# A hybrid RWKV-7 / RG-LRU layer with a Strassen MLP on one core: splits of the features spread over a pair's steps with four rooms, weights loaded by halves, and another issue order at the change of stages and in the last group

## The chip, the cores and the metric

One Trainium2 chip, one of its eight cores. The time is device time in microseconds of one launch, the median of several runs. TensorE (PE) multiplies matrices into PSUM, VectorE (DVE) and ScalarE (ACT) work on tiles, GpSimd (POOL) does elementwise work on tiles outside PSUM, SyncE (SP) issues nearly all transfers. Each of them takes its instructions in program order.

## What is computed

One trunk layer over 128 context tokens and 1024 latent tokens, all float32. The change touches its last part, the MLP, whose hidden width is 4096 over a model width of 1024:

```python
x = x + gate1 * rms_norm(y, lp['g_post_mix'])
h = rms_norm(x, lp['g_pre_mlp']) * (1.0 + scale2) + shift2
f = jnp.square(jax.nn.relu(jnp.einsum('btd,df->btf', h, lp['w_mlp1'])))
f = jnp.einsum('btf,fd->btd', f, lp['w_mlp2'])
x = x + gate2 * rms_norm(f, lp['g_post_mlp'])
```

Before it stand an input projection, a bidirectional delta-rule recurrence on 8 heads, a bidirectional gated linear recurrence on 512 channels and an output projection; they take the first 950 us and are not touched, but for one number (the size of GpSimd's descriptor ring).

## The kernel before

Every operand of a matmul is split in two parts of reduced precision, a high one (`H`, a copy by ACT) and the rest (`L`, a subtraction by DVE, or by GpSimd in the second product); a product is three matmuls (HH, HL, LH). To save matmuls, both MLP products use a Strassen-Winograd scheme with seven products instead of eight, so sums of blocks are formed and split too.

**First product.** The 32 blocks of 128 hidden units come in 16 pairs. Pairs 0 and 1 go through `plain` (no Strassen), pairs 2 to 15 through `strassen(p, hooks)`: 11 steps of 12 matmuls over three blocks of 384 tokens, in the order of `STEPS` (pair 15: `STEPZ`). After some steps ACT copies a partial sum out of PSUM (`t1`, `u2`, `u4`, line 2221), or `store` (2106) evacuates a finished block into `ft`: where a partial sum has to be added DVE does that first (2113), then ACT takes Relu (2115) and Square (2116). After each step the functions hung up for it run, `for fn in hooks.get(s_, ())`; they form the program order of ACT, DVE and SP. Three kinds hang there:
- `next_pair(p + 1)`: the weights of the next pair. `w_sums` (2175) forms block sums on DVE, `w_split` (2187) splits one of eight operands (ACT copy, DVE subtraction); `S4`'s sum stands in `w_split` itself. `w1_pair` (2096) loads the raw weights, two tiles of 512 KB, two pairs ahead, after step 10.
- `f_next(p - 1)` and `f_own(p)`: the features of the pair before and of this one. `f_sum` (2124) forms S1 to S4 on DVE, `f_split` (2131) splits an operand into a room of the ring `fs` (three rooms) and SP stores it to `Fd` in DRAM with two transfers of 256 KB; `c_split` (2141) does the same for the context part.
- `late_load`, `late_mm`, `late_out`: the last part of the modulation, in pairs 3 to 10.

PSUM has eight banks: tags g, m and G two each, s and P one each. Step 6 adds to the bank that `u2` was copied from after step 4; step 8 adds to the bank G that `store` reads after step 6.

**Second product.** Eight groups of two pairs (`mlp2`, 2368): first the context tile (tile 8) in two halves, `("c", 0)` and `("c", 1)`, then four quads (`QUAD`) of two token tiles in seven steps (`STEP2`), 6 matmuls a step. Hooks are named by quad and step. `f_load` fetches a quad's features from `Fd` into one of two pairs of buffers, `w_load` raw weights, `w_s` and `w_t` split and subtract them. `take` (2332) adds a step's result to the accumulator: by ACT for a first use in group 0 (2334), else by DVE (2336).

**Last group.** While group 7 runs, the gate of the second normalisation is built (`Gate.load`: two rows, then `mw` by quarters in two rooms; `Gate.make`: two additions and products on DVE, 1740 and 1741), `x1_load` fetches the residual of a tile into one of seven rooms, and each finished tile is normalised: `finish_a` (ACT), `finish_b` (DVE 2356, GpSimd 2358), its store, and the load of the residual seven tiles on, which needs the room that the store reads.

## Time and profile before

| | |
|---|---|
| runs, median | 1770.04 us |
| runs, lowest and highest of 3 | 1762.03, 1775.36 us |
| the profiled execution | 1776.04 us, its span 1774.3 us |
| mean granted TensorE clock of it | 0.964 |
| first product by Strassen (pairs 2 to 15) | from 994.3 to 1363.4 us |
| second product, eight groups | from 1366.2 to 1774.3 us |

The span runs from the first to the last instruction. Times below are microseconds from its start. PE clock 1.00 is 2.4 GHz; parts of a stretch at 1.2 GHz lower its mean. A matmul's record is longer than the distance to the next one, since they overlap; the distances of starts count.

### The profile page before, as it was taken

The page shows a single profiled execution, that of the slowest core. Times are in us where ns is not written, and L with a number is a line of the kernel's source. Part 1 is how long each engine was busy: PE and PEld are TensorE (multiplying, and loading weights), DVE is VectorE, ACT ScalarE, POOL GpSimd, SP SyncE. Part 2 cuts the span into 40 slices and gives each one's busy share as a digit, 9 for nine tenths or more (in the row PEclk, how much of TensorE's full clock was granted, in tenths as well). Part 3 has the DMA queues.
Part 4 walks back from the last instruction along what each step waited for, and adds up shares of the span by engine and source line. Part 5 has one row for each costly group of instructions (what it writes and reads, how often), then busy time and mean ns, then how long its engine had stood idle before and what let it go on. Part 6 is the DMA issues. An engine that isn't in the chain of part 4 may idle for free.

```text
span 1774.3 us, 33433 instructions
## 1 busy us (share of the span) xinstructions
PE 1604.7 (90%) x13035; PEld 1347.3 (76%) x13035; DVE 1103.0 (62%) x1884; ACT 805.1 (45%) x1549; POOL 518.3 (29%) x593
## 2 busy tenths in 40 slices
PE   6799988898999998699998999999998699999977
PEld 2688877787888766576777988999887578888855
DVE  3835585757976878665378756665666234444447
ACT  3734433443335676354356666665665322222202
POOL 3200368858012020212110000000000476666624
PEclk9999999989999999899999999999998899999989
DMA  9545857674556677989452766876676656555565
GB/s 310 194 131 136 210 137 187 169 185 116 146 131 139 154 175 182 216 206 256 147 213 78 211 194 193 237 220 183 185 225 234 226 219 221 222 221 223 221 234 206
DMA packets 436030, 341.22 MB, mean 192 GB/s; under 512 B 106392, under 2 KB 396384, under 8 KB 435872
## 3 DMA queue, kind: packets, MB, share of 16 engines
q1 hardware_dynamic: 433760, 331.53, 63.5%
q0 software_dynamic: 2112, 7.55, 1.3%
q8 instruction: 102, 1.67, 0.4%
q14 instruction: 56, 0.46, 0.1%
HBM read 214.72 MB, written 124.29 MB: 191 GB/s over the span
## 4 chain that ended last, share of the span: by engine, by line
PE 48%; DVE 17%; DMA 13%; POOL 7%; ACT 6%; issue 5%; SPq 3%; ACTq 0%; DVEq 0%; POOLq 0%
PE ps_g L2392 9%; DMA Fd<-fs 5%; PE ps_G L2392 4%; PE ps_g L531 3%; POOL ar L1028 3%; PE ps_g L532 3%; PE ps_g L533 3%; POOL ar L1024 3%; PE ps_m L2392 2%; PE ps_g L2216 2%; PE ps_g L1662 2%; PE ps_G L2216 2%; PE ps_P L2216 2%; PE ps_G L1503 1%; DVE fs L2135 1%
## 5 line engine op out<-in xcount | busy, mean ns | idle before, releaser
L531 PE MATMUL ps_g<-hH,wH 128*128 128x384 f32 x552 | 208.2, 377 | 2.6 <-DVE hH L270 1.9
L532 PE MATMUL ps_g<-hL,wH 128*128 128x384 f32 x552 | 190.7, 345 | 6.2 <-DVE hL L484 5.6
L533 PE MATMUL ps_g<-hH,wL 128*128 128x384 f32 x552 | 189.1, 343 | 0.0
L2304 POOL TENSOR_TENSOR sL<-w2r,sL 128x512 fp32r<-128x512 f32 x8 | 10.4, 1304 | 490.0 <-ACT sL L2303 490.0
L2336 DVE TENSOR_TENSOR acc<-ps_g,acc 128x512 f32<-128x512 f32 x116 | 80.2, 691 | 92.2 <-PE ps_g L2392 87.2
L531 PEld LDWEIGHTS ps_g<-hH,wH 128*128 128x128 f32 x552 | 107.0, 194 | 18.4 <-issue 8.4
L2216 PE MATMUL ps_P<-h2H,ws 128*128 128x384 f32 x432 | 119.0, 336 | 0.0
L532 PEld LDWEIGHTS ps_g<-hL,wH 128*128 128x128 f32 x552 | 107.2, 194 | 10.7 <-DVE hL L484 9.4
L2392 PE MATMUL ps_g<-sH,fT 128*128 128x512 f32 x408 | 109.2, 399 | 5.1 <-DVE acc L2336 5.1
L533 PEld LDWEIGHTS ps_g<-hH,wL 128*128 128x128 f32 x552 | 106.8, 193 | 0.0
L2392 PEld LDWEIGHTS ps_g<-sH,fT 128*128 128x128 f32 x408 | 77.4, 190 | 24.4 <-DVE acc L2336 5.8
L1024 POOL TENSOR_TENSOR ar<-ar 128x252 f32<-128x252 f32 (+22 forms) x124 | 82.5, 665 | 43.4 <-DMA ar<-NAd 21.0
L1028 POOL TENSOR_TENSOR ar<-ar 128x252 f32<-128x252 f32 (+22 forms) x124 | 86.9, 701 | 9.3
L2216 PE MATMUL ps_g<-oT,ws 128*128 128x384 f32 x336 | 67.8, 353 | 16.1 <-ACT u L2221 16.1
L2216 PEld LDWEIGHTS ps_P<-h2H,ws 128*128 128x128 f32 x432 | 79.4, 189 | 0.0
L2216 PEld LDWEIGHTS ps_g<-oT,ws 128*128 128x128 f32 x336 | 61.2, 198 | 19.8 <-ACT u L2221 19.6
L2216 PE MATMUL ps_G<-oT,ws 128*128 128x384 f32 x336 | 65.1, 342 | 11.0 <-DVE ft L2113 11.0
L2392 PE MATMUL ps_G<-sL,fT 128*128 128x512 f32 x252 | 71.4, 405 | 1.6 <-ACT acc L2334 1.3
L2216 PE MATMUL ps_P<-h2L,ws 128*128 128x384 f32 x216 | 72.6, 336 | 0.0
L1539 DVE TENSOR_TENSOR SV<-ps_m,Dt 64x256 f32<-64x256 f32 x136 | 57.1, 421 | 24.6 <-PE ps_m L1534 21.6
L2135 DVE TENSOR_TENSOR fs<-fS,fs 128x512 fp32r<-128x512 f32 x64 | 43.9, 687 | 43.2 <-ACT fs L2134 42.2
L2194 DVE TENSOR_TENSOR ws<-w1r,ws 128x512 fp32r<-128x512 f32 x56 | 38.4, 689 | 51.2 <-ACT ws L2193 51.2
(523 smaller groups left out, 4167.4 us busy)
## 6 DMA issues: line engine op xcount, KB each, us to landing
Fd<-fs SPq DMA_DIRECT2D x224, 256.0 KB
fT<-Fd SPq DMA_DIRECT2D x64, 896.0 KB
KGd<-ar SPq DMA_DIRECT2D x96, 192.0 KB
r<-KGd SPq DMA_DIRECT2D x36, 512.0 KB
mw<-in_w_mod_dram SPq DMA_DIRECT2D x64, 256.0 KB
w1r<-in_w_mlp_dram SPq DMA_DIRECT2D x32, 512.0 KB
w2r<-in_w_mlp_dram SPq DMA_DIRECT2D x31, 512.0 KB
raw<-in_w_in_dram SPq DMA_DIRECT2D x26, 512.0 KB
```

Source lines behind the costliest of these rows:

```text
L531: T.matmul(ps, wH[:, k, :], hH[b][:, k, :], start=(k == 0), stop=False)
L532: T.matmul(ps, wH[:, k, :], hL[b][:, k, :], start=False, stop=False)
L533: T.matmul(ps, wL[:, k, :], hH[b][:, k, :], start=False, stop=(k == 7))
L1024: E.tensor_tensor(out=t, in0=X[:, :, 0:m, j:j + 1].to_broadcast([128, 2, m, w]), in1=n[:, :, j % 8:j % 8 + 1, j + 1:32].to_broadcast([128, ...
L1028: E.tensor_tensor(out=X[:, :, 0:m, j + 1:32], in0=X[:, :, 0:m, j + 1:32], in1=t, op=ALU.subtract)
L1539: Q.add("V", cv(256), lambda e=e, ks=ks: V.tensor_tensor(out=SV[n][(s + 1) % NSV][ks, e], in0=x["S"][ks], in1=dv[ks], op=ALU.mult), r=[("S ...
L1662: T.matmul(z["ps"], y["t"][:, q // 2, k], wo_t[4 + k][q % 2][:, hs_], start=first, stop=last and stop)
L2135: V.tensor_tensor(out=t[:, 1], in0=f_raw(x), in1=t[:, 0].bitcast(F32), op=ALU.subtract)
L2194: V.tensor_tensor(out=w[:, 1], in0=ssum[p][x], in1=w[:, 0].bitcast(F32), op=ALU.subtract)
L2216: T.matmul(ps[ch], w[:, qw, k], h[q][:, k, :], start=(new and k == n == 0), stop=(k == 3 and n == 2), skip_group_check=True)
L2336: V.tensor_tensor(out=acc_(i, h), in0=ps, in1=acc_(i, h), op=ALU.add)
L2392: T.matmul(ps[ch], f[:, OPI[fx], qf], w[:, qw], start=(new and e == n == 0), stop=(e == 1 and n == 2), skip_group_check=True)
```

## The change

- The ring `fs` has four rooms instead of three. The 4 KB a partition come from `dynamic_dma_scratch_size`, 8192 to 4096, the ring for transfers that GpSimd issues.
- `f_next` and `f_own` hang the seven feature splits at other steps: at most one a step in the steady pairs, S3 at step 8 and A11 at step 9.
- `store` with an addition returns Relu and Square as a function, `rest`, which `strassen` calls after the step's hooks.
- The weights' sum `S4` moves from `w_split` (step 10) to `w_sums` (step 3).
- `w1_pair` becomes two calls of `w1_half`, the first after step 5, the second after step 10.
- In pair 15 the two loads of `w2` stand at steps 0 and 2, the feature splits are spread likewise, and A11 of pair 15 is split after the pair.
- In group 0 the next group's first splits start after step 2 of the first quad instead of after the context halves; in the other groups nothing changes.
- In the last group the gate's additions stand at steps 4 and 5 of the first quad and 2 and 3 of the second, one `x1_load` at each of the seven steps of the first quad, and `finish_a` and `finish_b` follow two tables, `FA` and `FH`.

The diff, with unchanged lines left out:

```diff
@@ -2051,21 +2051,21 @@
             if m == 2:
-                for q in {1: (0, 1), 2: (2, 3, 4), 0: (5, 7)}[b]:
-                    for fn in f_next(0)[q][0 if q > 1 else 3 if q == 0 else 2:]:
+                for q in {1: (2, 3), 2: (4, 5, 6), 0: (7, 8)}[b]:
+                    for fn in f_next(0)[q]:
                         fn()
...
                         fn()
-                    w_sums(NPL, 0, 1, 2)
+                    w_sums(NPL, 0, 1, 2, 3)
                 for i in range(0, 3) if b == 2 else range(3, 6):
...
         elif m == 1:
-            for fn in f_next(0)[0] + f_next(0)[1][0:2]:
+            for fn in f_next(0)[0] + f_next(0)[1]:
                 fn()
@@ -2093,11 +2093,17 @@
+    def w1_half(p, i):
+        if i == 0:
+            w1r[p] = [wp.tile([128, 8, 128], F32, tag="raw", name="w1r", bufs=1)]
+        else:
+            w1r[p].append(dp.tile([128, 8, 128], F32, tag="q0", name="w1r2") if p > NPL else
+                          wsp.tile([128, 8, 128], F32, tag="ws", name="w1r2", bufs=4))
+        SY.dma_start(out=w1r[p][i], in_=w1v[:, :, 128 * (2 * p + i):128 * (2 * p + i) + 128])
+
     def w1_pair(p):
-        w1r[p] = [wp.tile([128, 8, 128], F32, tag="raw", name="w1r", bufs=1),
-                  dp.tile([128, 8, 128], F32, tag="q0", name="w1r2") if p > NPL else wsp.tile([128, 8, 128], F32, tag="ws", name="w1r2", bufs=4)]
         for i in range(2):
-            SY.dma_start(out=w1r[p][i], in_=w1v[:, :, 128 * (2 * p + i):128 * (2 * p + i) + 128])
+            w1_half(p, i)
@@ -2111,9 +2117,10 @@
             V.tensor_tensor(out=f, in0=add, in1=src, op=ALU.add)
-            src = f
-        S.activation(out=f, in_=src, func=AF.Relu)
-        S.activation(out=f, in_=f, func=AF.Square)
+        S_ = lambda: [S.activation(out=f, in_=x, func=fn) for x, fn in ((src if add is None else f, AF.Relu), (f, AF.Square))]
+        if add is not None:
+            return S_
+        S_()
@@ -2130,7 +2137,7 @@
-        t = dp.tile([128, 2, 512], F32R, tag="fs", name="fs", bufs=3)
+        t = dp.tile([128, 2, 512], F32R, tag="fs", name="fs", bufs=4)
         S.activation(out=t[:, 0], in_=f_raw(x), func=AF.Copy)
@@ -2146,13 +2153,13 @@
-        return {4: [lambda: f_split(p, "A11")], 5: [lambda: c_split(p, 0)]}
+        return {5: [lambda: c_split(p, 0)], 9: [lambda: f_split(p, "A11")]}
...
         sp, su = (lambda x: lambda: f_split(p, x)), (lambda x: lambda: f_sum(x))
-        return {0: [sp("A12"), sp("A22"), su("S1")], 1: [su("S2"), su("S3"), sp("S1")], 2: [sp("S2")], 3: [sp("S3")],
-                4: [su("S4")], 5: [sp("S4")], 7: [lambda: c_split(p, 1)]}
+        return {0: [su("S1"), sp("A12")], 1: [su("S2"), su("S3")], 2: [sp("A22")], 3: [sp("S2")], 4: [su("S4")], 5: [sp("S1")],
+                6: [sp("S4")], 7: [lambda: c_split(p, 1)], 8: [sp("S3")]}
@@ -2178,17 +2185,16 @@
             s3 = dp.tile([128, 4, 128], F32, tag="s3", name="s3")
-            ssum[p] = {"A11": a11, "A12": a12, "A21": a21, "A22": a22, "S1": t[:, 0], "S2": t[:, 1], "S3": s3}
+            s4 = dp.tile([128, 4, 128], F32, tag="s4", name="s4")
+            ssum[p] = {"A11": a11, "A12": a12, "A21": a21, "A22": a22, "S1": t[:, 0], "S2": t[:, 1], "S3": s3, "S4": s4}
         x = ssum[p]
         for n in ns:
-            o_, p_, q_, op = (("S1", a21, a22, ALU.add), ("S2", x["S1"], a11, ALU.subtract), ("S3", a11, a21, ALU.subtract))[n]
+            o_, p_, q_, op = (("S1", a21, a22, ALU.add), ("S2", x["S1"], a11, ALU.subtract), ("S3", a11, a21, ALU.subtract),
+                              ("S4", a12, x["S2"], ALU.subtract))[n]
             V.tensor_tensor(out=x[o_], in0=p_, in1=q_, op=op)
...
         x = WORD[i]
-        if x == "S4":
-            s4 = ssum[p][x] = dp.tile([128, 4, 128], F32, tag="s4", name="s4")
-            V.tensor_tensor(out=s4, in0=ssum[p]["A12"], in1=ssum[p]["S2"], op=ALU.subtract)
         w = wop[p, x] = slot8().rearrange("p q (k f) -> p q k f", f=128)
@@ -2215,15 +2221,17 @@
                              skip_group_check=True)
-            e = wx, hx
+            e, rest = (wx, hx), None
             d = {("A11", "B11"): t1, ("S2", "T2"): u2, ("S1", "T1"): u4}.get(e)
...
                 i, b, add = EV[e]
-                store(p, i, b, ps[ch if e != ("S1", "T1") else "z"], {1: t1, 2: u2, 4: u4}.get(add))
+                rest = store(p, i, b, ps[ch if e != ("S1", "T1") else "z"], {1: t1, 2: u2, 4: u4}.get(add))
             for fn in hooks.get(s_, ()):
                 fn()
+            if rest:
+                rest()
     EV = {("A12", "B21"): (0, 0, 1), ("A12", "E2"): (0, 2, 0), ("S1", "T1"): (1, 1, 4), ("A22", "T4"): (1, 0, 2), ("A22", "E2"): (1, 2, 0),
@@ -2231,7 +2239,7 @@
         su = lambda *n: lambda: w_sums(p, *n)
-        return {2: [su(0), sp_(0)], 3: [su(1, 2)], 4: [sp_(1)], 5: [sp_(2)], 6: [sp_(3)], 7: [sp_(4)], 8: [sp_(5)], 10: [sp_(6), sp_(7)]}
+        return {2: [su(0), sp_(0)], 3: [su(1, 2, 3)], 4: [sp_(1)], 5: [sp_(2)], 6: [sp_(3)], 7: [sp_(4)], 8: [sp_(5)], 10: [sp_(6), sp_(7)]}
@@ -2379,7 +2387,6 @@
             run(hooks, ("c", h))
-        fin = [8]
         for u, (i, j) in enumerate(QUAD):
@@ -2393,19 +2400,16 @@
                 run(hooks, (u, s_))
-                if last:
-                    if u == 3 and s_ == 5:
-                        finish_a(j)
-                    if s_ == 0:
-                        for q in fin:
-                            finish_a(q)
-                    if s_ in (2, 4) and s_ // 2 <= len(fin):
-                        finish_b(fin[s_ // 2 - 1])
-            fin = [j, i]
+                if last and (u, s_) in FH:
+                    finish_b(FH[u, s_])
+                if last and (u, s_) in FA:
+                    finish_a(FA[u, s_])
         if last:
-            finish_a(QUAD[3][0])
-            finish_b(QUAD[3][1])
-            finish_b(QUAD[3][0])
+            finish_a(6)
+            finish_b(7)
+            finish_b(6)
+    FH = {(1, 4): 8, (1, 6): 3, (2, 1): 0, (2, 3): 4, (2, 6): 1, (3, 2): 5, (3, 4): 2}
+    FA = {(0, 6): 8, (1, 2): 3, (1, 5): 0, (2, 0): 4, (2, 2): 1, (3, 0): 5, (3, 1): 2, (3, 5): 7}
@@ -2422,11 +2426,10 @@
         tt = lambda e, x: lambda: w_t(n, e, x)
-        add("c", 0, sp(0, "B11"))
-        add(0, 0, sp(0, "B12"))
-        add(0, 2, sp(0, "B21"))
-        add(0, 4, sp(0, "B22"))
-        add(0, 5, tt(0, "T1"))
+        z = (("c", 0), (0, 0), (0, 2), (0, 4), (0, 5)) if g else ((0, 2), (0, 3), (0, 4), (0, 5), (0, 6))
+        for k, x in zip(z, ("B11", "B12", "B21", "B22")):
+            add(*k, sp(0, x))
+        add(*z[4], tt(0, "T1"))
         add(1, 0, sp(0, "T1"), tt(0, "T2"))
@@ -2451,7 +2454,8 @@
         if p + 2 < NP:
-            hooks[10] = hooks[10] + [lambda p=p: w1_pair(p + 2)]
+            hooks[5] = hooks[5] + [lambda p=p: w1_half(p + 2, 0)]
+            hooks[10] = hooks[10] + [lambda p=p: w1_half(p + 2, 1)]
         u = p - NPL - 1
@@ -2476,26 +2480,26 @@
             fsp, fsu = (lambda x: lambda: f_split(p - 1, x)), (lambda x: lambda: f_sum(x))
-            hooks = {0: [lambda: w_load(0, 0), lambda: w_load(0, 1)] + f_next(p - 1)[0],
-                     1: f_next(p - 1)[1],
-                     2: [fsp("S2"), rooms, sp(0, "B22")],
-                     3: [fsp("S3"), tt(0, "T1"), sp(0, "B11")],
-                     4: [fsu("S4"), tt(0, "T2"), fsp("S4")],
-                     5: [sp(0, "T2"), sp(0, "B21"), sp(0, "T1")],
-                     6: [lambda: c_split(p - 1, 1), lambda: f_load(0, 0),
-                         lambda: c_load(0)],
+            fc1 = lambda: c_split(p - 1, 1)
+            fn_ = f_next(p - 1)
+            hooks = {0: [lambda: w_load(0, 0)] + fn_[0],
+                     1: fn_[1] + [fsp("A22")],
+                     2: [rooms, sp(0, "B22"), lambda: w_load(0, 1)],
+                     3: [fsp("S2"), tt(0, "T1"), sp(0, "B11")],
+                     4: [fsu("S4"), tt(0, "T2"), fsp("S1")],
+                     5: [sp(0, "T2"), sp(0, "B21"), sp(0, "T1"), lambda: c_split(p, 0)],
+                     6: [fsp("S4"), fc1, lambda: f_load(0, 0), lambda: c_load(0)],
                      7: [sp(1, "B11"), rooms2, sp(1, "B21"), tt(0, "T4"), sp(0, "B12")],
                      8: [rooms3, sp(1, "B12"), sp(1, "B22"), sp(0, "T4")],
-                     9: [tt(0, "T3"), sp(0, "T3"), lambda: f_load(0, 1)],
+                     9: [fsp("S3"), tt(0, "T3"), sp(0, "T3"), lambda: f_load(0, 1)],
                      10: [tt(1, "T1"), tt(1, "T2"), sp(1, "T2")]}
-            for k, v in f_own(p).items():
-                hooks[k] = hooks[k] + v
         strassen(p, hooks)
...
     w_s(0, 1, "T4", V)
+    f_split(NP - 1, "A11")
     for k, v in f_next(NP - 1).items():
@@ -2516,11 +2520,13 @@
                 g2.load(h)
+            hk = lambda u, s_, fn: hooks.setdefault((u, s_), []).append(fn)
+            for h in range(2):
+                hk(0, 4 + h, lambda h=h: g2.make(h))
+                hk(0, 4 + h, lambda h=h: g2.load(h + 2))
+                hk(1, 2 + h, lambda h=h: g2.make(h + 2))
             for n in range(7):
-                x1_load(n)
-            for h in range(2):
-                hooks.setdefault(("c", h), []).extend([lambda h=h: g2.make(h), lambda h=h: g2.load(h + 2)])
-                hooks.setdefault((0, h), []).insert(0, lambda h=h: g2.make(h + 2))
+                hk(0, n, lambda n=n: x1_load(n))
         mlp2(g, hooks)
@@ -2570,7 +2576,7 @@
-    nc = bacc.Bacc("TRN2", target_bir_lowering=False, num_devices=1, dynamic_dma_scratch_size=8192)
+    nc = bacc.Bacc("TRN2", target_bir_lowering=False, num_devices=1, dynamic_dma_scratch_size=4096)
     arrays, a, o = {}, {}, {}
```

## Rows read from the trace of the kernel before

**Rows 1.** Windows: from:to, length, busy us (instructions) by engine, PE clock, DMA share, GB/s.
```profile
1021.35:1330.83 309.48, 290.89 (x1729) 276.58 (x1729) 198.82 (x352) 190.12 (x384) 0.00 (x0) 1.00 0.70 206
...
1278.30:1303.60 25.30, 23.51 (x135) 22.87 (x134) 16.46 (x29) 15.88 (x32) 0.00 (x0) 1.00 0.67 198
...
1341.00:1366.00 25.00, 17.14 (x86) 16.50 (x84) 14.74 (x26) 14.52 (x30) 0.00 (x0) 0.86 0.95 314
...
1476.10:1520.80 44.70, 44.70 (x194) 36.05 (x193) 20.76 (x30) 9.34 (x16) 30.64 (x25) 1.00 0.61 223
...
1699.70:1774.30 74.60, 51.07 (x193) 38.64 (x191) 44.17 (x68) 13.22 (x28) 26.51 (x18) 0.86 0.61 229
```

**Rows 2.** The chain that ended last, in time: start, us, engine or transfer, line.
```profile
1010.13 4.21 PE ps_g L2216 x12
...
1019.27 2.08 PE ps_P L2216 x12
...
1328.76 2.08 PE ps_P L2216 x12
...
1384.32 4.70 DMA w2r<-in_w_mlp_dram
...
1701.46 8.11 DMA mw<-in_b_mod_dram
...
1744.39 8.28 DMA fT<-Fd
```

**Rows 3.** Line 2216, steps 0 and 10: shortest/median/longest ns, first and last start.
```profile
L2216 PE MATMUL ps_g<-h2H,ws x224: 331/335/338, 994.3 to 1363.0; 128*128 128x384 f32 x112
```

**Rows 4.** Timeline of TensorE in pair 4: start, us, line, tile.
```profile
1053.46 0.64 PE L382 MATMUL ps_s<-mw,sT 128*32 128x128 f32 x16
...
1060.48 0.38 PE L2090 MATMUL ps_s<-mw,sel 128*2 128x128 f32 x2
```

**Rows 5.** Waits from 994 to 1340 us: who for whom, us in all, times, longest.
```profile
ACT ft L2115 <- DVE ft L2113: 54.6, 39, 2.1
...
PE ps_G L2216 <- DVE ft L2113: 11.0, 12, 1.0
...
ACT fs L2134 <- DMA Fd<-fs: 12.4, 19, 1.9
PE ps_g L2216 <- ACT u L2221: 10.8, 10, 3.2
```

**Rows 6.** Timelines of ACT and DVE in pair 12.
```profile
1270.24 0.47 ACT L2221 ACTIVATE u<-ps_g 128x384 f32<-128x384 f32 x1
...
1275.39 0.55 DVE L2113 TENSOR_TENSOR ft<-u,ps_G 128x384 f32<-128x384 f32 x1
```

**Rows 7.** Timeline of TensorE at the change of stages; idle before in brackets.
```profile
1352.76 4.21 PE L2216 MATMUL ps_g<-oT,ws 128*128 128x384 f32 x12 [5.25 <-ACT u L2221]
...
1366.19 4.41 PE L2379 MATMUL ps_s<-s,fT 128*128 128x512 f32 x12 [2.80 <-DMA fT<-Fc]
...
1390.70 0.79 PE L2392 MATMUL ps_g<-sL,fT 128*128 128x512 f32 x1 [14.34 <-ACT acc L2334]
```

**Rows 8.** Timeline of ACT there.
```profile
1389.04 0.63 ACT L2303 ACTIVATE sL<-w2r 128x512 fp32r<-128x512 f32 x1 [6.76 <-DMA w2r<-in_w_mlp_dram]
```

**Rows 9.** Waits from 1698 us to the end.
```profile
DVE fzH L1740 <- DMA mw<-in_b_mod_dram: 13.0, 2, 6.6
...
PE ps_g L2392 <- DVE acc L2336: 10.7, 2, 5.6
...
PE ps_g L2392 <- DMA fT<-Fd: 0.7, 1, 0.7
```

**Rows 10.** Timelines of SP and GpSimd in the last group.
```profile
1728.20 0.34 SPq L2362 DMA_DIRECT2D out_dram<-fzH  x1
1732.66 0.33 SPq L2347 DMA_DIRECT2D fzH<-X1d  x1
...
1725.25 2.92 POOL L2358 TENSOR_TENSOR fzH<-acc,fzH 128x512 f32<-128x512 f32 x2 [22.45 <-DVE acc L2356]
```

**Rows 11.** The page's list of DMA queues: packets, MB, share.
```profile
q0 software_dynamic: 2112, 7.55, 1.3%
```

## The prediction, made before the changed kernel ran

> **What bounds the kernel now.** I read the busy times by stage first. In the first MLP product the matmul engine works 290.9 us of 309.5; in a middle group of the second it works 44.7 us of 44.7, so there nothing can be won; in the last group 51.1 of 74.6, at a granted clock of 0.86 [rows 1]. So TensorE sets the end throughout, and what counts are its holes and the stretches at the lower of its two clock levels (1.2 GHz instead of 2.4). The profiled execution took 1776.04 us: its span of 1774.3 and 1.7 around it. The median of the runs is 1770.04.
>
> The chain of work gives the size of the holes. Pair 2 starts at 994.3; its tenth step starts at 1019.27, that of pair 14 at 1328.76 [rows 2, 3]. Twelve pairs take 309.49 us, 25.8 each. A step is 12 matmuls in 2.08 us [rows 2], a pair 11 steps or 22.9. In eight of the pairs (3 to 10) the late part of the modulation adds about 0.64 and 0.38 [rows 4]. So 12 x 22.88 + 8 x 1.0 = 282.6, and 26.9 us are holes. Pair 2 needs 24.97 for nine steps worth 18.7: 6.25 lost, since a stall there is followed by 12 matmuls in 4.21 us, half the rate [rows 2].
>
> The list of waits says who makes them: TensorE waits 10.8 us for ACT's copy `u` (ten times) and 11.0 for DVE's addition into `ft` (twelve times) [rows 5]. Each is one step behind a hand-over: after step 4 ACT must copy `u2` before step 6; after step 6 ACT copies `u4` and DVE adds `z` before step 8. One step, 2.08 us, is the slack. The copy itself takes 0.47 and the addition 0.55 [rows 6]. They come late because both queues run in order and what stands ahead was itself waiting: ACT's Relu for DVE's addition (54.6 us, 39 times), ACT's split for its room, i.e. for the store of an older `fs` (12.4 us, 19 times) [rows 5]. In a pair ACT is busy 15.9 us and DVE 16.5 of 25.3 [rows 1]: neither is full, it is the order.
>
> **The first product, after the change.** No operation is added or taken away in a pair; 14 split stores, 7 splits, 6 evacuations stay. I laid both queues out over the steps by the means of [rows 1] (15.88/32 = 0.50 us for ACT, 16.46/29 = 0.57 for DVE), t = 0 at the pair's first matmul, steps ending at 2.08(s+1)+0.2. ACT: the last two weight splits end at 2.2, because `S4`'s subtraction has moved to step 3 and ACT no longer waits for it; A12 3.3, A22 3.8, weight 4.9; the deferred Relu and Square follow the addition at 7.0 and end at 8.0; step 3's evacuation and S2 10.0; step 4 ends at 10.6, so `u2` is copied at 11.1, needed at 12.5. Then A12 of the weights, c, S1, S2 of the weights end at 12.8; `u4` comes at 14.76 to 15.24. DVE by then has done its last earlier work at 15.05 and adds until 15.8; step 8 may start at 16.6. Margins 1.4 and 0.8 us: both holes close. Rooms: with seven splits spread over 22.9 us and four rooms, a room is wanted again no sooner than 9 us after its store is issued (S2 at 10.7, A11 of the same pair at 22), against at most 12.4 us waited in 19 places now. The deferral moves only the order; what waits behind a deferred Relu is the next step's evacuation, which is 0.5 us later than that. SP issues the same stores. I leave 0.3 us a pair for hiccups (3.6 in all, between 0 and 10): gain 26.9 - 3.6 = 23.3. Pair 2 loses its stall by the same; there is one more DVE subtraction (0.57) ahead of its first weights, hidden behind step 0's first matmuls. I take 5.4 of 6.25.
>
> **Weights by halves.** The first half goes out at step 5, behind S1's stores on SP, once A12's split of the old raw tile is done: two steps ahead of nothing that needs it. The second goes out as before after the last two splits, now at t = 3.0, and DVE wants it at 7.6 (`S1` of the next weights). The nearest row for 512 KB behind stores is 4.70 us [rows 2]: it lands at 7.7. Behind that wait on DVE stand a weight split, S2, three sums and the addition of step 6, with 0.8 us to spare. So it costs nothing up to a landing of 5.4 us, and 1 us a pair for each us beyond.
>
> **Change of stages.** In the last pair TensorE waits 5.25 us for `u2`, then runs a step in 4.21 instead of 2.08 [rows 7]. ACT stood behind rooms and weight copies. Now S2 and S1 are the only splits ahead and find rooms, so 7.4 us go; the wait for the transfer of `Fc` (2.80) stays, since the same transfers stand ahead of it and the transfer engines are 95% busy at 314 GB/s there [rows 1, 7]. After it comes the hole of 14.34 us: the first `B11` split of the next group stands in ACT's queue ahead of two evacuations, and waits for `w2r`, issued at 1384.32 and landed 4.70 later [rows 2, 7, 8]. The change puts it behind step 2, so TensorE restarts when ACT is through the last splits, at about 1383.3 by the old times (the wait in [rows 8] begins 6.76 before 1389.04, at 1382.3, then two copies of 0.5), instead of 1390.70: 7.4 us. If the 6.9 us saved in the pair (7.4 less the A11 copy that moved here) pass through ACT and the transfers, 14.3. Transfers are near full, so I take the middle, 11 for all of it (5 if the weights' load becomes the end, 14.3). `B11`'s wait now has steps 2 to 4 as cover, some 7 us at the lower clock.
>
> **The last group.** TensorE is idle 10.7 us behind two evacuations of DVE that stand after the gate's additions, which wait 13.0 us for `mw` [rows 9]; add 0.7 for `fT`, and 51.1 - 44.7 = 6.4 at the lower clock [rows 1]: 17.8 in all. The additions move from the context tile to steps 4 and 5 of the first quad, which end 12.6 and 14 us after the group's start (192 matmuls in 44.7 us make a step of 6 in 1.40), while the first load lands 8.11 us after its issue at 1701.46 [rows 2], 9.9 after that start: these waits go. The second two are issued as the first are added, 14.7 and 16.8 after the start, and wanted at 20.3: by the same 8.11, 2.5 us late. What is late next is SP. The transfer of the last quad's `fT` is issued after (1,6), and now the store of tile 8 and the load of its successor stand ahead of it on SP. `finish_b(8)` comes 0.7 us after step (1,4) ends; DVE 1.6, GpSimd 2.9, and from the store's issue to the load's 4.46 (1728.20 to 1732.66) [rows 10]: 10 us after (1,4). The quad is wanted nine steps of 1.40 after it, 12.6; the pair of transfers takes 8.28 [rows 2]. So TensorE waits 5.7, and a wait of 5.25 was followed by a step at half rate [rows 7]; with the tiles less crowded, 3 and nothing. Between 7.8 and 3 I take 6.3, and 2 for `mw` and for the third quad's transfer, which now stands behind it and six `x1` loads: 17.8 - 8.3 = 9.5 (2 to 17.8). The tail behind the last matmul (74.6 - 51.1 - 10.7 - 0.7 = 12.1) has the same calls in the same order: nothing. The Trainium skill (DMA: Bandwidth & Descriptors, section Bandwidth) measures 341 GB/s for 1 MB; by it `fT`'s 1.8 MB would take an estimated 5.4 us instead of the 8.28 of the row, and the sum would be some 3 us better.
>
> **GpSimd's transfer ring** is halved to pay for the fourth room. Its transfers are 2112 packets, 7.55 MB [rows 11], none in the MLP. Below nothing, above one or two waits of the size of an `mw` or `fT` transfer (8.28), some 10 us; I take nothing, as they are far apart.
>
> **Sum.** 23.3 + 5.4 + 11 + 9.5 = 49.2: 1776.0 - 49.2 = 1726.8 for an execution like the profiled one, 1720.8 from the median, which is 6 us below it. I count from the middle of the two, 1773, here and below: 1724.
>
> **Rivals.**
> A, only the room is cured: the waits for `u` go, those for `ft` stay, since DVE's addition also stands behind splits that wait for ACT. For it: 54.6 us of Relu waits are not about rooms. Against: the layout gives the addition 0.8 us. Gain 11 less, 38.2: 1735. The Trainium skill (Perfetto Trace Analysis, section Optimization Strategy) says consistent bubbles can mean too little room for the next tile; read alone, that would be this case, and the trace bears it out for 12.4 us only [rows 5].
> B, transfers take the place of the waits in the two dense stretches: 4 instead of 11 and 2 instead of 9.5. For it: 95% busy, and `f_load` behind `x1` on SP. Against: the whole last group averages 0.61 [rows 1]. 23.3 + 5.4 + 4 + 2 = 34.7: 1738.
> C, better: all is covered: 26.9 + 6.2 + 14.3 + 17.8 = 65: 1708.
> D, the other side: the second half of the weights is late in every pair. All twelve pairs lose what it exceeds 5.4 us by; the 49 us are gone at 9.5 us, and 1% more at 11. For it: transfers of 8.28 exist. Against: only one store of 0.5 MB is ahead. At 11 us it is 12 x 5.6 - 49 = 18 slower: 1791.
>
> **How the numbers follow.** My sum 0.52, A 0.14, B 0.16, C 0.10, D 0.04, and 0.04 that the change does no more than stir (the first product stays at 25.5 a pair): about 1765. The range takes C's 1708 and B's 1738, widened by the 6 us between the profiled execution and the median below and by the ring's 10 us above: 1702 to 1750. About 1% is what a measurement of this kernel can tell from no change. Faster by more (below 1752): all of the sum, A and C, most of B: 0.88. Within: 0.08. Slower: 0.04.
>
> **What would show it.** Right: pairs of 23 to 24 us, no wait of TensorE for `u` or `ft`, no ACT wait for `Fd`; TensorE restarting in the first group before any `w2r` wait; DVE without a wait for `mw`; one hole before the last quad. Wrong: DVE waiting for `w1r` at `sS` (D), holes of 1 us before `ps_G` (A), a hole before the third quad too (B), GpSimd's queue waiting in the first 900 us (ring).

## The result, and the profile after

The changed kernel takes 1720.57 us (median of four runs, 1718.16 to 1722.11); the kernel before, beside it, 1770.92. The ratio is 0.9721, with a 95% interval of 0.968 to 0.976. The prediction was 1724, with a range of 1702 to 1750.

The two profiled executions lie further apart, 1776.04 and 1720.11: 55.9 us. I cut both at the same starts of matmul steps.

| stretch | before | after | gain | forecast |
|---|---|---|---|---|
| up to the start of pair 2 | 994.3 | 990.5 | 3.8 | 0 |
| nine steps of pair 2 | 24.97 | 19.71 | 5.3 | 5.4 |
| twelve pairs, from there to the same step of pair 14 | 309.49 | 285.23 | 24.3 | 23.3 |
| from there to the first context tile | 37.43 | 31.68 | 5.8 | } 11 |
| group 0 of the second product | 65.1 | 60.9 | 4.2 | } 11 |
| groups 1 to 6 | 268.4 | 268.4 | 0 | 0 |
| last group and tail | 74.6 | 61.8 | 12.8 | 9.5 |

The first row lies before all that was changed, but for a few splits of the plain pairs and GpSimd's ring, and the same stretch ended between 985.6 and 995.8 in the twelve runs below: it is the spread between executions, no gain of the change.

The windows of the kernel after (from:to, length, busy us and instructions by engine, clock, DMA share, GB/s), in order the twelve pairs, the change of stages, group 0, a middle group, the last group:
```profile
1010.21:1295.44 285.23, 285.23 (x1730) 277.86 (x1729) 201.09 (x353) 190.91 (x385) 0.00 (x0) 1.00 0.77 225
1295.44:1327.12 31.68, 27.10 (x156) 26.81 (x156) 23.02 (x39) 21.87 (x45) 0.00 (x0) 0.98 0.86 273
1327.12:1388.04 60.92, 51.51 (x192) 39.96 (x193) 19.38 (x31) 24.46 (x44) 26.77 (x22) 0.90 0.73 253
1522.26:1566.96 44.70, 44.70 (x193) 36.07 (x192) 20.75 (x30) 9.34 (x16) 30.59 (x25) 1.00 0.60 224
1656.48:1718.30 61.82, 46.90 (x193) 35.21 (x191) 44.39 (x68) 13.42 (x28) 26.50 (x18) 0.94 0.78 276
```
TensorE is busy in all 285.23 us of the first row, where [rows 1] had 290.89 of 309.48. VectorE's and ScalarE's work there is what it was within 3 us; what changed is where it stands. The list of waits of the kernel after, 990 to 1310 us (who for whom, us in all, times, longest), is to be held against [rows 5]:
```profile
ACT ft L2120 <- DVE ft L2119: 39.4, 27, 2.8
ACT u L2227 <- PE ps_g L2222: 34.7, 25, 2.4
...
DVE ft L2119 <- PE ps_G L2222: 2.7, 12, 0.2
...
ACT fs L2141 <- DMA Fd<-fs: 0.3, 1, 0.3
PE ps_G L2222 <- DVE ft L2119: 0.2, 1, 0.2
DVE sS L2194 <- DMA w1r<-in_w_mlp_dram: 0.2, 1, 0.2
```
The direction has turned. TensorE waited 10.8 us for the copy `u`; now the copy waits 34.7 us for TensorE. TensorE's wait for the addition fell from 11.0 to 0.2, ScalarE's for a room from 12.4 to 0.3. ScalarE still waits 39.4 us for the addition (54.6 before), and that costs nothing: a wait is no loss as long as what stands behind it is not wanted yet.

What holes are left stand at the change of stages. TensorE's timeline there (start, us, line, tile, idle before in brackets), to be held against [rows 7]:
```profile
1327.12 5.46 PE L2387 MATMUL ps_s<-s,fT 128*128 128x512 f32 x12 [4.58 <-DMA fT<-Fc]
1342.22 1.18 PE L2399 MATMUL ps_g<-sL,fT 128*128 128x512 f32 x3 [3.99 <-ACT acc L2342]
1351.99 0.97 PE L2399 MATMUL ps_G<-sL,fT 128*128 128x512 f32 x3 [3.75 <-ACT acc L2342]
```
And ScalarE's timeline before the second of them and at the last:
```profile
1340.08 0.63 ACT L2141 ACTIVATE fs<-fS 128x512 fp32r<-128x512 f32 x1 [0.98 <-DMA Fd<-fs]
...
1350.82 0.63 ACT L2311 ACTIVATE sL<-w2r 128x512 fp32r<-128x512 f32 x1 [5.51 <-DMA w2r<-in_w_mlp_dram]
1351.36 0.58 ACT L2342 ACTIVATE acc<-ps_G 128x512 f32<-128x512 f32 x1
```
The hole of 14.34 us is now two, 3.99 and 3.75. The first ends as forecast, when ScalarE is through the last splits, before any wait for `w2r`; but here, past the pairs, splits still wait for a room, about 1 us each. ScalarE's wait for `w2r` is still there (6.76 before, 5.51 now), with an evacuation behind it; steps run in front of it, but not enough of them.

In the last group, TensorE's timeline at the first steps of the third and of the last quad, then SP's between them, then the two loads of features in the chain:
```profile
1684.75 0.96 PE L2399 MATMUL ps_g<-s,fT 128*128 128x512 f32 x3 [1.24 <-DMA fT<-Fd]
...
1696.42 0.96 PE L2399 MATMUL ps_g<-s,fT 128*128 128x512 f32 x3 [0.24 <-DMA fT<-Fd]
```
```profile
1684.72 0.34 SPq L2370 DMA_DIRECT2D out_dram<-fzH  x1
1687.36 0.32 SPq L2355 DMA_DIRECT2D fzH<-X1d  x1
1687.77 0.86 SPq L2326 DMA_DIRECT2D fT<-Fd  x2
```
```profile
1675.25 9.46 DMA fT<-Fd
1688.25 8.13 DMA fT<-Fd
```
The matmuls end at 1706.14, 49.66 us after the group's start, of which 44.7 are work. VectorE no longer waits for `mw`.

### The profile page after: what moved, and what is told of

It reads as the page before. It is cut to its first block, busy times and chain, and to the rows that moved or that the text cites. A ratio compares the mean times of both kernels' runs of the same rounds, so it can differ in the third digit from the quotient of the medians.

```text
span 1718.3 us, 33433 instructions
## 1 busy us (share of the span) xinstructions
PE 1591.1 (93%) x13035; PEld 1341.4 (78%) x13035; DVE 1107.6 (64%) x1884; ACT 803.4 (47%) x1549; POOL 518.5 (30%) x593
## 4 chain that ended last, share of the span: by engine, by line
PE 68%; DVE 13%; DMA 7%; POOL 4%; ACT 4%; issue 3%; SPq 1%; DVEq 0%; POOLq 0%; ACTq 0%
PE ps_g L2399 9%; PE ps_g L2222 6%; PE ps_P L2222 6%; PE ps_G L2399 4%; PE ps_g L531 4%; PE ps_g L532 3%; PE ps_g L533 3%; PE ps_G L2222 3%; PE ps_g L1662 3%; PE ps_m L2399 2%; PE ps_m L1534 2%; PE ps_G L1503 2%; PE ps_m L2222 2%; DMA wm<-in_w_mod_dram 2%; PE ps_G L1519 2%
## 5 line engine op out<-in xcount | busy, mean ns | idle before, releaser
L2120 ACT ACTIVATE ft<-ft 128x384 f32<-128x384 f32 x138 | 72.3, 524 | 42.4 <-DVE ft L2119 39.4
L1539 DVE TENSOR_TENSOR SV<-ps_m,Dt 64x256 f32<-64x256 f32 x136 | 57.1, 421 | 23.3 <-PE ps_m L1534 17.0
L2344 DVE TENSOR_TENSOR acc<-ps_G,acc 128x512 f32<-128x512 f32 x60 | 41.4, 690 | 38.4 <-PE ps_G L2399 38.4
L2311 ACT ACTIVATE sL<-tt 128x512 fp32r<-128x512 f32 x31 | 19.6, 632 | 94.1 <-POOL tt L2305 62.6
L2222 PE MATMUL ps_g<-oT,ws 128*128 128x384 f32 x336 | 63.0, 336 | 0.0
```

Source lines behind the costliest of these rows:

```text
L1539: Q.add("V", cv(256), lambda e=e, ks=ks: V.tensor_tensor(out=SV[n][(s + 1) % NSV][ks, e], in0=x["S"][ks], in1=dv[ks], op=ALU.mult), r=[("S ...
L2120: S_ = lambda: [S.activation(out=f, in_=x, func=fn) for x, fn in ((src if add is None else f, AF.Relu), (f, AF.Square))]
L2222: T.matmul(ps[ch], w[:, qw, k], h[q][:, k, :], start=(new and k == n == 0), stop=(k == 3 and n == 2), skip_group_check=True)
L2344: V.tensor_tensor(out=acc_(i, h), in0=ps, in1=acc_(i, h), op=ALU.add)
```

## The experiments

Twelve kernels. A figure such as "336.6 from pair 2 to the context" is the distance between two starts on TensorE's timeline of that kernel's profile. Ratios are to the kernel before, which ran beside each.

### Rooms alone

The kernel before with two lines of the change:
```
-        t = dp.tile([128, 2, 512], F32R, tag="fs", name="fs", bufs=3)
+        t = dp.tile([128, 2, 512], F32R, tag="fs", name="fs", bufs=4)
-    ... dynamic_dma_scratch_size=8192)
+    ... dynamic_dma_scratch_size=4096)
```


> The kernel before with four rooms for fs instead of three and GpSimd's ring halved; the order untouched. Theory (the order of the queues makes the holes): the 12.4 us of room waits go, but u2's copy comes only about 0.5 us earlier in a steady pair, and the holes before ps_G stay: a pair takes about 25.2 instead of 25.8, pair 2 and the last pair get most of their long waits back (5 and 3 us); 1755 us, ratio 0.991. Rival A (too few rooms make the holes): all waits for u go, pairs near 24.5, 1743 us, ratio 0.984. Ring: the first 950 us no longer than before by more than 3 us.

Measured: 1757.05 us, ratio 0.993 (0.9908 to 0.9951); 355.9 from pair 2 to the context, 371.9 before. Its waits, 1000 to 1310 us:
```profile
PE ps_G L2216 <- DVE ft L2113: 7.2, 13, 0.8
...
PE ps_g L2216 <- ACT u L2221: 4.2, 5, 2.6
...
ACT fs L2134 <- DMA Fd<-fs: 0.5, 2, 0.3
```
ScalarE's wait for rooms is gone (12.4 to 0.5), and with it most of TensorE's wait for `u`; the addition is still late in each of thirteen pairs. The time is that of my theory, and the rival's 1743 is out, but the picture of what is left is the one that rival A drew.

### Rooms taken back, deferral taken back

The changed kernel with three rooms and the full ring:


> The changed kernel with three rooms and the full ring again; its order kept. Theory: in the new order a room is wanted again 6 us or more after its store, so pairs stay within 0.3 us of the changed kernel's 23.77 and only the run of splits after the last pair loses some 2 us: 1723 us, ratio 0.973. Rival A: without the fourth room ACT waits for stores in each pair and pairs go back to 25 or more: 1740 us or above, ratio 0.983 or above.

Measured: 1718.91, ratio 0.9708 (0.9683 to 0.9733); 336.5 from pair 2 to the context, 336.6 in the changed kernel. In the new order the fourth room is worth nothing, and the 2 us that the theory gave it after the last pair don't show either. The halved ring shows no cost either: GpSimd's transfers lie before pair 2, and that stretch ended at 989.1 with the full ring and at 990.5 with the half.

The changed kernel with Relu and Square back at their place (`S_()` called in `store` always):


> The changed kernel with Relu and Square issued at once after DVE's addition instead of after the step's hooks. Theory: by the layout u2's copy still has 0.9 us and the addition of step 6 0.8 us to spare, so the deferral adds next to nothing: pairs 23.8 to 24.1, 1722 us (1720 to 1727). Rival E (the Relu waits of 54.6 us were the cause): pairs of 25 or more, 1738 us.

Measured: 1726.02, ratio 0.9748 (0.9729 to 0.9768); 338.2. The steady pairs are as long without the deferral (the table below); of the 1.6 us, 1.1 lie in pair 2 (24.8 against 23.7). The medians lie 5.5 us apart and the two sets of runs don't overlap (1724.53 to 1726.59, and 1718.16 to 1722.11). The profiles put the rest before pair 2 and into group 0, within what those stretches vary by in kernels that don't differ there, so that it is not shown to be the deferral's.

### The weights: when they are asked for, and where S4 is summed

`S4`'s sum back at step 10, the halves kept:
```
-3: [su(1, 2, 3)]
+3: [su(1, 2)]
...
+        if x == "S4":
+            w_sums(p, 3)
         w = wop[p, x] = slot8()...
```


> The changed kernel with the weights' sum S4 formed again in step 10 just before its split. Theory: ACT's wait for it (1.4 us) ends at t = 3.6 of the next pair, in front of work that has until 6.4, so no hole from ACT; but the second half of the weights goes out 1.4 us later and lands at about 9.1 if it takes 4.70 us, 1.5 after DVE wants it, of which 0.8 are spare: 0 to 0.7 us a pair, 1720 to 1729 us. Rival D's size: if landing takes less than 4 us nothing is seen; if it takes more than 6, over 2 us a pair, 1745 us.

Measured: 1796.92, ratio 1.0141 (1.0109 to 1.0173): slower than the kernel before, by less than 2% but clear of the noise. From pair 2 to the context 417.5. The expectation (1720 to 1729, the rival 1745) missed this by 68 us at least. Its waits, 1000 to 1310 us, then SP's timeline and VectorE's from the end of one pair into the next:
```profile
ACT fs L2141 <- DMA Fd<-fs: 47.1, 10, 5.9
DVE sS L2194 <- DMA w1r<-in_w_mlp_dram: 46.1, 11, 5.9
...
PE ps_G L2224 <- DVE ft L2119: 31.1, 10, 4.4
```
```profile
1101.56 1.26 SPq L2145 DMA_DIRECT2D Fd<-fs  x2
1112.39 0.37 SPq L2102 DMA_DIRECT2D w1r<-in_w_mlp_dram  x1
1112.86 1.23 SPq L2145 DMA_DIRECT2D Fd<-fs  x2
1114.17 1.38 SPq L2152 DMA_DIRECT2D Fc<-fc  x1
1115.64 2.64 SPq L2145 DMA_DIRECT2D Fd<-fs  x4
1118.38 0.76 SPq L2102 DMA_DIRECT2D w1r<-in_w_mlp_dram  x1
```
```profile
1111.68 0.68 DVE L2194 TENSOR_TENSOR s<-w1r,sS 128x512 f32<-128x512 f32 x1
...
1123.84 0.69 DVE L2194 TENSOR_TENSOR sS<-w1r 128x512 f32<-128x512 f32 x1 [4.08 <-DMA w1r<-in_w_mlp_dram]
```
`S4` is A12 less S2, and A12 lies in the raw tile that the first half is loaded into. SP issues nothing from 1102.8 to 1112.39; VectorE's last reading of the raw tile, the sum of `S4`, ends at 1112.36, and the load leaves at once. Behind it had stood six stores of splits and one of the context. So ScalarE waits for rooms, the second half leaves only 6 us after the first, and VectorE, with the addition of step 6 in its queue, waits 4.08 us for it. That is rival D's wait, by a way that the prediction did not name. Two more kernels show that it is SP's standing and not the place of the sum: both halves after step 10, once with `S4` early (the diff), once with it late.
```
-            hooks[5] = hooks[5] + [lambda p=p: w1_half(p + 2, 0)]
-            hooks[10] = hooks[10] + [lambda p=p: w1_half(p + 2, 1)]
+            hooks[10] = hooks[10] + [lambda p=p: w1_pair(p + 2)]
```


> The changed kernel with both halves of a pair's raw weights issued after step 10, S4's sum left at step 3. Theory: the second half then lands some 1.7 us later, at about 9.4 of the next pair by 4.70 us for the first; DVE wants it at 7.6 and has 0.8 to spare, so about 1 us a pair over twelve pairs: 1732 us (1722 to 1735), with DVE waiting for w1r at sS. Rival (loading by halves is worth nothing): pairs as in the changed kernel, 1720 us, no such wait.

Measured: 1718.54, ratio 0.9689 (0.9657 to 0.9721); 338.2. My theory fell, the rival held. The waits show the lateness, and that it is absorbed (1000 to 1310 us):
```profile
ACT ws L2199 <- DMA w1r<-in_w_mlp_dram: 29.2, 12, 3.8
...
PE ps_G L2222 <- DVE ft L2119: 0.5, 1, 0.5
```


> Both undone together: S4's sum in step 10 and both halves of the weights behind it, as in the kernel before. The run e4 left the first half at step 5 while its room is read until step 10, so SP stood still for half a pair. Theory (SP's standing made e4 slow, not S4's place): without it the transfers of features flow again; loads leave at 4.4 and the second half lands at about 10.8, 3.2 late less 0.8: 2.4 a pair, 1749 us (1735 to 1755), no ACT wait for Fd. Rival (S4's place itself makes ACT late): 1790 us as e4.

Measured: 1719.33, ratio 0.9701 (0.9666 to 0.9736); 339.0, no wait for `Fd` left. Again the expectation was wrong (1749): VectorE waits for the second half in each of thirteen pairs, 1000 to 1310 us, and pairs 3 to 14 are no longer for it.
```profile
DVE sS L2194 <- DMA w1r<-in_w_mlp_dram: 13.8, 13, 2.0
```
The reason for the kernel that lost 76 us is confirmed: `S4`'s place alone does nothing, nor do the halves alone. Only a load at the head of SP whose room is still read does.

### The order of the splits, alone and taken away

Everything in the pairs put back but the order (three rooms, no deferral, both halves and `S4` at step 10):


> The changed kernel with everything of its product pairs put back except the standing of the features' splits: three rooms (and the full ring), no deferral of Relu and Square, both weight halves after step 10, S4's weight sum at step 10. The change of stages and the last group stay changed. Theory (the order of the splits carries the pairs' gain, the rest is worth the 1 to 2 us of the deferral): start of pair 2 to the first context tile 338 to 341 us (changed kernel 336.6, before 371.9), time 1718 to 1727. Rival (the small parts only look worthless one at a time, since each covers for another): 345 to 356, time 1728 to 1740.

Measured: 1727.66, ratio 0.9753 (0.973 to 0.9777); 341.9. The order alone brings 30.0 of the 35.3 us between 371.9 and 336.6. Both figures fall just between the two forecasts.

The converse: all parts kept, and the splits in the order of before:
```
-        return {5: [lambda: c_split(p, 0)], 9: [lambda: f_split(p, "A11")]}
+        return {4: [lambda: f_split(p, "A11")], 5: [lambda: c_split(p, 0)]}
-        return {0: [su("S1"), sp("A12")], 1: [su("S2"), su("S3")], 2: [sp("A22")], ...
+        return {0: [sp("A12"), sp("A22"), su("S1")], 1: [su("S2"), su("S3"), sp("S1")], ...
```


> The converse: the changed kernel, all its parts kept, but the features' splits in the order of before (in the plain pairs and in pairs 2 to 14; pair 15 as changed). Theory (the order carries the gain): start of pair 2 to the first context tile 350 to 356 us, like the kernel before with four rooms (355.9), VectorE's and ScalarE's waits in a ring (ScalarE for VectorE's ft, TensorE for ps_G) back, time 1734 to 1740. Rival (deferral, halves and rooms together carry it whatever the order): 337 to 342, time 1720 to 1725.

Measured: 1717.72, ratio 0.9705 (0.9677 to 0.9734); 338.4. The theory on record, that the order carries the gain, fell: without it the twelve pairs lose nothing, and the stretch 1.8 us, which lie in pair 2 (25.7 against 23.7). Its waits, 1000 to 1310 us:
```profile
ACT ft L2120 <- DVE ft L2119: 24.6, 39, 1.2
...
ACT u L2227 <- PE ps_g L2222: 8.0, 20, 0.5
...
PE ps_G L2222 <- DVE ft L2119: 1.4, 1, 1.4
```
The copy waits for TensorE here too, but with less in hand, 8.0 us against 34.7. The steps themselves say it most plainly. From TensorE's timelines, the median length of steps 5 and 7 (to the next step's start) and the mean pair, in the eight pairs that carry the late part of the modulation and in the four that don't:
```
                                     pairs 3 to 10            pairs 11 to 14
                                  step 5  step 7  pair      step 5  step 7  pair
before                             2.62    3.22   26.02      3.25    3.04   25.33
rooms alone                        2.19    2.65   24.87      2.63    3.02   24.62
order of splits alone              2.19    2.08   24.20      2.33    2.43   23.62
changed, splits in the old order   2.19    2.08   24.20      2.08    2.08   22.91
changed, three rooms               2.19    2.08   24.20      2.08    2.08   22.91
changed, no deferral               2.19    2.08   24.20      2.08    2.08   22.91
changed                            2.19    2.08   24.20      2.08    2.08   22.91
```
Nearly all of a pair's loss sits in two steps: step 5, whose length holds the wait of step 6 for the copy of `u2`, and step 7, whose length holds the wait of step 8 for the addition. The rooms alone cure step 5 and half of step 7 in the pairs with the modulation; in the last four they cure half of step 5 and nothing of step 7. The order alone cures both in the first eight and leaves 0.7 us a pair in the last four. The rest of the change, put on top of the rooms, cures both everywhere, in the old order too. So no one of order, fourth room, deferral and halves has a price of its own here: taken away one at a time, each costs the twelve pairs nothing and the stretch up to the context 0 to 2 us, while together they gain 24 in the twelve pairs. `S4`'s earlier sum is the exception: as long as the halves are kept, it can't be left out.

Which member of "the rest" cures step 7 in the old order, the deferral, the halves or the earlier sum of `S4`, was not separated.

### Change of stages and last group

Group 0's first weight splits where they stood, the rest changed:


> The changed kernel with group 0's first splits of the next weights at the context halves again. Theory: TensorE restarts only after w2r has landed (some 9 us later than now), but then has no second hole of 3.75: group 0 takes 66 to 68 us instead of 60.9, 1726 us (1724 to 1729). Rival (the splits behind the pairs bound the restart): no change, 1720 us.

Measured: 1723.72, ratio 0.9725 (0.9693 to 0.9758); group 0 65.3, a little under the 66 to 68 expected, and the rival (no change) is out by the trace. The runs' intervals overlap with the changed kernel's (0.968 to 0.976), so the price is read from group 0 alone: 65.1 to 65.7 in the three profiles with the old place, 58.0 to 62.4 in the nine with the new that differ in nothing else there. TensorE's timeline there has the long hole back in place of 3.99 and 3.75:
```profile
1347.85 1.65 PE L2399 MATMUL ps_g<-sL,fT 128*128 128x512 f32 x3 [13.82 <-ACT acc L2342]
```
The last group in the order of before, the rest changed:


> The changed kernel with the last group's order of before (gate's additions at the context tile, seven residual loads ahead, old places of the finishing steps). Theory: the last group takes 74.6 to 76.3 us again instead of 61.8: 1734 us, DVE waiting 13 us for mw. Rival B (transfers bound that group anyway): under 66 us, 1724 us.

Measured: 1733.46, ratio 0.9776 (0.9748 to 0.9804); last group 75.6, as the theory had it (74.6 to 76.3). Its waits from 1655 us to the end:
```profile
DVE fzH L1740 <- DMA mw<-in_b_mod_dram: 13.1, 2, 6.5
...
PE ps_g L2400 <- DVE acc L2344: 10.7, 2, 5.7
```
These are [rows 9] again, 13.0 and 10.7. This part's price is its own: the last group takes 74.6, 76.3 and 75.6 us in the three profiles with the old order (before, rooms alone, this one), and 61.7 to 64.5 in the ten with the changed one, whatever the pairs are like.

### Two attempts to get more

In the first, the raw half of group 1's weights is asked for before the last pair's remaining splits, into the same tile (the lines that leave out its later load are not shown):
```
+    wpre.append(wp.tile([128, D], F32, tag="raw", name="w2r", bufs=1))
+    SY.dma_start(out=wpre[0], in_=a["w_mlp2"][0, 512:640])
     w_s(0, 1, "T1", V)
```


> The changed kernel with one load moved: the first half of group 1's second-layer weights is asked for right after the last product pair's loop, ahead of that pair's last feature splits, instead of in group 0. Theory (ScalarE's wait of 5.51 us for this load makes TensorE's next hole of 3.75 us in group 0): the wait and that hole go, group 0 falls from 60.9 to 56 to 58 us, time 1715 to 1718. Rival (the load only takes its place in the queue ahead of the features' stores, so that TensorE's wait of 4.58 us for the context's features grows by the 1.5 to 2 us that its half megabyte takes): group 0 60 to 62, time 1719 to 1722.

Measured: 1717.39, ratio 0.9695 (0.9673 to 0.9717). TensorE's timeline, the same three places:
```profile
1328.02 4.63 PE L2389 MATMUL ps_s<-s,fT 128*128 128x512 f32 x12 [5.93 <-DMA fT<-Fc]
1342.36 1.65 PE L2401 MATMUL ps_g<-sL,fT 128*128 128x512 f32 x3 [4.13 <-ACT acc L2344]
...
1359.58 0.96 PE L2401 MATMUL ps_G<-sL,fT 128*128 128x512 f32 x3 [1.62 <-ACT acc L2344]
```
Group 0 falls from 60.9 to 56.6 and the third hole from 3.75 to 1.62, as the theory had it. The first grows from 4.58 to 5.93, but that is not shown to be the rival's cause: the same hole lies between 4.3 and 6.5 in kernels without this edit, and is 4.01 in the next one, which has it. From pair 2 to group 1 that is 394.6 against 397.5. The time fits a gain of 3 us over the changed kernel, but the two intervals overlap (0.9673 to 0.9717, and 0.968 to 0.976), and group 0 lay between 58.0 and 62.4 in kernels that do not differ there. I don't call it faster.

In the second, three loads of `x1` are also moved behind the third quad's features:
```
-                hk(0, n, lambda n=n: x1_load(n))
+                hk(*((0, n) if n < 4 else (1, n)), lambda n=n: x1_load(n))
```


> The kernel of the run above, and in the last group the loads of x1 numbers 4 to 6 hung behind the second quad's steps 4 to 6 instead of the first quad's. Theory (they stand on SP ahead of the third quad's features and make TensorE's 1.24 us wait for them): that wait goes, last group from 61.8 to 60.5 to 61, time 1 us below the run above. Rival (the transfers are only moved against the stores and the last quad's features, which then come late): last quad's wait grows from 0.24 to over 1, last group 61.5 to 63.

Measured: 1718.59, ratio 0.9705 (0.968 to 0.9731); last group 64.9, more than either side expected and just outside the 61.7 to 64.5 of the kernels with the order unmoved. The third quad's wait for features is gone, and the last quad pays; TensorE there:
```profile
1689.53 0.96 PE L2401 MATMUL ps_g<-s,fT 128*128 128x512 f32 x3 [1.78 <-DMA fT<-Fd]
```
That wait is 0.24 in the changed kernel and 0.61 in the run above. The matmuls of the group end 52.75 us after its start, 49.66 in the changed kernel. The rival's way is the one seen, the loads only moved to where the next features want the transfers, though the medians of the two attempts can't be told apart.

## Why the prediction was right, point by point

**Twelve pairs: 23.3 forecast, 24.3 measured.** The mechanism was the one named: nothing added, both engines with time to spare, what they do standing in the wrong place. The layout written out over the steps holds in the profile. In the pair whose step 0 starts at 1230.71, `u2` is copied at t = 10.6 (forecast 10.6 to 11.1), `u4` at 14.8 (14.76), the addition ends at 15.9 (15.8), the second half goes out at 2.5 (3.0) and VectorE comes to it at 7.5 (7.6). The size is partly luck, since two terms were off and cancel. The 0.3 us a pair left for hiccups (3.6) was not needed: there are none. And the holes were 24.3, not 26.9, and all of them closed: the late part of the modulation costs its pairs 1.29 us (24.20 against 22.91), where the prediction took 1.0 from the records of [rows 4], and a pair without it takes 22.91 and not 22.88. Pair 2 came at 5.3 (5.4).

**What the forecast did not see: the gain is there twice.** I laid out the whole change and it closed both holes; that says nothing of which part does it. In the eight pairs with the modulation either the order alone or the rest without the order is enough; in the last four the rest is enough and the order alone nearly so. My expectations that followed the layout part by part failed (the order taken away: 1734 to 1740 expected, 1717.72 measured). The margins of 1.4 and 0.8 us are not the sum of the parts' margins.

**Rival A** asked for the addition to stay late once ScalarE no longer waits for rooms. It is what the rooms alone do; the changed kernel has more. **The Trainium skill** (Perfetto Trace Analysis, section Optimization Strategy) says consistent bubbles can mean too little room for the next tile. Here more room is worth 0.7% in the old order and nothing measurable in the new (336.5 and 336.6).

**Weights by halves: nothing forecast, nothing measured.** One wait of 0.2 us in thirteen pairs. **Rival D** did not come, but the kernel with `S4` late shows what it looks like: 1797. The forecast named the wait, the second half being late, and not its cause; what kept it away is one line of the change, the sum of `S4` at step 3, whose use lies on SP and not in ScalarE's queue, where the prediction had put it. Its price was wrong too, 1 us a pair for each us that VectorE waits beyond the 0.8 to spare: with both halves and `S4` late VectorE waits 13.8 us in thirteen pairs, up to 2.0 in one, and none of pairs 3 to 14 is longer.

**Change of stages: 11 forecast, 9.9 measured,** made up otherwise. Forecast were 7.4 in the pair, the wait for `Fc` as it was, and 3.6 in group 0 as the middle of 0 and 6.9. Measured are 5.8 up to the context, because the wait for `Fc` grew from 2.80 to 4.58, and 4.2 in group 0. The step that failed is the sentence that the wait for `w2r` has steps 2 to 4 as cover: they cover a part, and 3.75 us of TensorE's time stand behind it. That the transfers are near full there was right, 0.86 busy and 273 GB/s over the stretch; that this alone made the wait for `Fc` longer is not shown.

**Last group: 9.5 forecast, 12.8 measured.** Mis-sized is the term for the last quad's features, 6.3 against 0.24. Two things made it small. The store and the load on SP stand 2.64 us apart, not 4.46 (why is not shown), so the features are asked for 8.9 us after step (1,4) ends (1678.89), not 10; and the work up to there is itself slowed, with four waits of 0.26, 1.24, 0.30 and 0.56, 2.4 us in all, and longer steps beside them, so that the last is wanted 16.4 us after that step, not 12.6. A loss that I added to the others was partly spent inside them. The transfer pair took 8.13 and 9.46 us, as the row of before said (8.28). The term of 2 for the third quad was 1.24. The estimate of 5.4 us by the Trainium skill (DMA: Bandwidth & Descriptors, section Bandwidth) does not agree with these two durations; its figure is measured on transfers that GpSimd issues, and these are SP's. That the pair shares the engines with other transfers, which together moved 306 GB/s in the group's first 50 us, is the likely reason and was not tested.

**Rivals B and C.** B had 4 and 2 for the two dense stretches; they gave 9.9 and 12.8. One sign that was set down for it came, the hole before the third quad, but of 1.24 us. C had everything covered, 65; in the pairs all was, but there were only 24.3 to win, and holes stayed in group 0.

**The ring:** nothing, as forecast (full ring 1718.91, half ring 1720.57).

**Sum.** Over the changed stretches the profiles give 52.2 (5.3 + 24.3 + 5.8 + 4.2 + 12.8, before rounding) and the medians 50.35, against 49.2. That the sum is nearer than its terms is luck: 1.1 too much at the change of stages stands against 3.3 too little in the last group. Of the 3.4 us between 1724 and 1720.57, 2.1 are the starting point (1773, where the runs beside it have 1770.92) and 1.2 the gain.

## What to carry to other kernels

When two in-order engines hand work to each other one step ahead of the matmuls, lay both queues out over the steps and compare with the hand-over that is wanted; here that gave the moments in a pair to within 0.5 us. Then do not price the parts one by one: cures of the same loop of waits replace each other, so a part that costs nothing when taken away may still be worth most of the gain when it is alone. And before a load is hung earlier on a queue that also carries stores, look for the last reader of its tile: if that comes after the load, the queue stands, and everything behind it.

## What the runs showed of the hardware

SP's transfers wait for their tile at the head of SP's queue and hold back all that follows: in the pair shown SP issued nothing for 9.6 us and then sent seven stores in a row, and that kernel is 76 us slower than the changed one. Of TensorE's clock the rows show this. Group 0 of the changed kernel, with holes of 4.58 us at its start and of 3.99 and 3.75 in it, ran at a granted clock of 0.90. The last group's first 50 us, with holes of up to 1.24 us, stayed at 1.00 in that kernel. Small holes are not always without this price: in the changed kernel with three rooms a hole of 0.49 us stood 2 us ahead of one of the same 1.24, the clock fell to 0.50, the lower level, right behind it, and the stretch ran at 0.97. TensorE's timeline there, then the windows of the stretch and of the fall:
```profile
1679.78 0.97 PE L2399 MATMUL ps_g<-sL,fT 128*128 128x512 f32 x3 [0.49 <-DMA fT<-Fd]
1681.98 0.96 PE L2399 MATMUL ps_g<-s,fT 128*128 128x512 f32 x3 [1.24 <-DMA fT<-Fd]
```
```profile
1653.28:1704.24 50.96, 48.20 (x193) 36.44 (x191) 36.64 (x59) 10.64 (x22) 20.90 (x15) 0.97 0.83 297
1682.80:1686.20 3.40, 3.40 (x10) 2.66 (x9) 1.35 (x3) 0.00 (x0) 2.29 (x2) 0.50 0.43 153
```
